# Low parts of the projections' weights: a subtraction on VectorE replaced by a negation on ScalarE and an accumulating transfer

## The chip, the cores and the metric

The kernel runs on one core of one Trainium2 chip. A core has a TensorE (PE, matrix products into PSUM banks), a VectorE (DVE), a ScalarE (ACT), a GpSimd (POOL) and a SyncE (SP), each with its own in-order instruction queue, and 16 DMA engines. The metric is the device time of one execution in microseconds, as the median of several runs.

## The reference

One layer of a hybrid block over 1024 tokens of width 1024. Two branches read the same RMS-normalised input; their gated sum is projected and added to the input, and a squared-ReLU MLP and a last RMSNorm follow.

```python
xn = rmsnorm(x, norm1_g[layer])
u = xn @ w_in[layer].astype(f32)
q_sb, k_sb, v_sb, f_raw, i_hg, q_hg, g_hg, gate_sb, gate_hg = jnp.split(u, list(c), axis=-1)
o_sb = stick_breaking_attention(split_heads(q_sb, SB_HEADS), ...)
...
o_hg = hgrn2_chunkwise(split_heads(jax.nn.silu(q_hg), HG_HEADS), ...)
...
merged = g_a * (o_sb @ w_o_sb[layer].astype(f32)) + g_b * (o_hg @ w_o_hg[layer].astype(f32))
h = x.astype(f32) + merged @ w_out[layer].astype(f32)
hn = rmsnorm(h, norm2_g[layer])
a = jnp.square(jax.nn.relu(hn @ w_ff1[layer].astype(f32)))
h = h + a @ w_ff2[layer].astype(f32)
```

Everything is float32, and the tolerance is that of float32.

## The kernel before

The large products are made in a rounded float32 format (`fp32r`). To keep the precision, each operand is split into a high part (the value rounded to that format) and a low part (the rest), and every product is made of three matmuls, high by high, high by low and low by high (`three`, line 466). The high part is a copy on ScalarE that rounds (`hi_copy`, line 133, recorded as L134). The low part is a subtraction on VectorE, raw minus high (`lo_sub`, line 136, recorded as L137). `hi_lo` (line 139) does both.

The weights of the projections come in units (class `Unit`, line 368). `Unit.load` (line 378) has SP load one or two raw tiles of 128x1024 float32 (512 KB) from HBM; `Unit.split` (line 390) makes a high and a low tile of each. The raw tiles lie in a pool with two buffers of the tag `raw`; high and low tiles of the narrow units have two buffers each (`whi`, `wlo`), those of the wide units (value, input and w_out projections) lie in the general slots. So a raw buffer can be loaded again only when the unit's split has read it, and a high or low buffer can be written again only when the matmuls of the unit two before have read it.

Jobs are queued in a `Stream` (line 413): the first job makes queries and keys of head 0 and the values of heads 0 to 3 (`first_job`, line 580); then come queries and keys of heads 1 to 7 (`wqk1` to `wqk7`, with `wv1` between), the recurrence's projections (`wf`, `wq`, `wi`, `wg` per head), 16 gate projections (`wg00` to `wg17`) with an output projection of the attention or the recurrence after every second one (`wo00` to `wo13`), and two jobs of w_out (`wout_job`, line 1035). When a job starts, `Stream.prefetch` (line 431) splits the next job's unit and loads the one after it. The tiles of a unit are named after it with h, l and r behind: `wo13h`, `wo13l`, `wo13r`.

The matmuls of the jobs fill the gaps of the main work on PE, whose order against the jobs is written out by hand: stick-breaking attention up to about 320 us (scores z, sigmoids `rm` and `bt`, a scan on VectorE at line 646, a product `bt`, transposes `pw`, their split into `wTh` and `wTl`, and the values `po`), then the levels and tails of the recurrence; from wg06 on the jobs run alone. In attention each head's queries are copied to the other half of the partitions by two DMAs issued from POOL (line 563, QH<-QH and QL<-QL). POOL also writes the small memsets at lines 631 and 676. A scheduler that knows the dependencies sets each engine's final order.

The tail of the kernel is the MLP, which makes its splits elsewhere and does not use `Unit`.

Of the kernel before, what the change touches and what calls it, by code (L numbers as in the profile page):

```python
# [14 lines left out]
ALU = mybir.AluOpType  # L15
# [24 lines left out]
def kernel(  # L40
# [19 lines left out]
    nc = tc.nc  # L60
# [14 lines left out]
    def slot(name, dt=F32):  # L75
        return spool.tile([P, 1024], dt, tag="s", name=name)
# [7 lines left out]
    def bank(name):  # L84
        return psum.tile([P, 512], F32, tag="p", name=name)
# [3 lines left out]
    class Lane:  # L89
        def __init__(self):  # L90
            self.ends = []
            self.last = None
            self.gates = ()
# [4 lines left out]
    def after(ins, earlier):  # L98
        if earlier is not None and earlier.ins is not ins.ins:
            tc.add_manual_dep(ins.ins, earlier.ins.name, NOSYNC, reason="issue order")  # L100
        return ins
# [26 lines left out]
    def load(dst, src):  # L128
        last_load[0] = after(nc.sync.dma_start(dst, src), last_load[0])
# [3 lines left out]
    def hi_copy(dst, src):  # L133
        after(nc.scalar.copy(dst, src), hold[0])  # L134

    def lo_sub(dst, src, hi):
        return nc.vector.tensor_tensor(out=dst, in0=src, in1=hi.bitcast(F32), op=ALU.subtract)  # L137

    def hi_lo(h, l, src):
        hi_copy(h, src)  # L140
        return lo_sub(l, src, h)
# [134 lines left out]
    class Quads:  # L276
# [42 lines left out]
        def split(self, i, kp, src, pr=0, n=4):  # L319
            if (i, kp) not in self.hl:  # L320
                self.hl[i, kp] = tuple(slot(f"sq{n_}{i}{kp}", F32R) for n_ in "hl")
            h, l = (self.part(t, pr, n) for t in self.hl[i, kp])
            self.last_lo = hi_lo(h, l, self.part(src, pr, n))
# [44 lines left out]
    class Unit:  # L368


        def __init__(self, name, pieces, wide=False):
            self.name = name
            self.pieces = pieces
            self.wide = wide
            self.raw = None
            self.hl = None

        def load(self):
            if self.raw is not None:
# [10 lines left out]
        def split(self):  # L390
            if self.hl is not None:
                return
            self.load()
            self.hl = []
            for i, r in enumerate(self.raw):
                if self.wide:
                    h = slot(f"{self.name}h{i}", F32R)
                    l = slot(f"{self.name}l{i}", F32R)
                else:
                    h = wpool.tile([P, 1024], F32R, tag="whi", name=f"{self.name}h{i}")  # L400
                    l = wpool.tile([P, 1024], F32R, tag="wlo", name=f"{self.name}l{i}")
                hi_lo(h, l, r)
                self.hl.append((h, l))

    def cols_unit(name, parts):

        dmas, c = [], 0
        for mat, c0, n in parts:
            dmas.append((c, n, mat[:, c0 : c0 + n].rearrange("(k p) c -> p k c", p=P)))
            c += n  # L410
        return Unit(name, [dmas])
# [54 lines left out]
    def three(ps, wh, wl, xh, xl, first, last, goes_on=False):  # L466
        matmul(ps, wh, xh, start=first, stop=False, skip_group_check=goes_on)
        matmul(ps, wh, xl, start=False, stop=False, skip_group_check=goes_on)
        matmul(ps, wl, xh, start=False, stop=last, skip_group_check=goes_on)

    def proj_half(ps, hl, mov, nk, half, wcol=lambda k: k * P):
        wh, wl = hl
        for kt in range(nk):
            c = wcol(kt)
            xh, xl = mov(kt, half)
            three(ps, wh[:, c : c + P], wl[:, c : c + P], xh, xl, kt == 0, kt == nk - 1)
            if kt % 2 == 1:
                yield
# [13 lines left out]
    def token_steps(name, unit, acts, tbs, epilogue):  # L492

        for tb in tbs:
            ps = bank(f"{name}_{tb}")[:, 0:256]
            for kt in range(KT):
                sh, sl = acts.stat(kt, tb)
                wh, wl = unit.hl[kt // 4]
                cs = slice((kt % 4) * 256, (kt % 4 + 1) * 256)
                three(ps, sh, sl, wh[:, cs], wl[:, cs], kt == 0, kt == KT - 1)  # L500
                if kt == 3:
                    yield
            epilogue(ps, tb)
            yield
# [31 lines left out]
    def v_epilogue(quad):  # L536


        def ep(ps, tb):
            if tb % 2 == 0:  # L540
                vt[quad, tb // 2] = slot(f"V{quad}_{tb // 2}", F32R)
            V = vt[quad, tb // 2].rearrange("p (t h s d) -> p t h s d", t=2, h=4, s=2)
            src = ps.rearrange("p (h d) -> p h d", h=4)
            hi_lo(V[:, tb % 2, :, 0, :], V[:, tb % 2, :, 1, :], src)

        return ep
# [20 lines left out]
    def v_unit(quad):  # L567
        return wide_unit(f"wv{quad}", W_IN, C_V + quad * 256)
# [7 lines left out]
    def qk_item(h):  # L576
        u = cols_unit(f"wqk{h}", [(W_IN, C_Q + h * DHS, DHS), (W_IN, C_K + h * DHS, DHS)])
        return f"pjqk{h}", u, qk_epilogue(h)

    def first_job():  # L580
        name, u_qk, ep = qk_item(0)
        u_v = v_unit(0)

        def body():
            v_ep = v_epilogue(0)
            for half in range(2):
                ps = bank(f"{name}_{half}")
                yield from proj_half(ps, u_qk.hl[0], xn.mov, KT, half)
                ep(ps, half)
                if half == 0:  # L590
                    u_v.split()
                    yield
                    st.prefetch()
                yield from token_steps("pjv0", u_v, xn, range(4 * half, 4 * half + 4), v_ep)

        return st.add([u_qk, u_v], body)

    j_qk = {0: first_job()}
    for h in range(1, NHS):
        j_qk[h] = proj_jobs([qk_item(h)], xn)  # L600
# [164 lines left out]
    for h in range(NHG):  # L765
        for key, c0, ep in (
# [6 lines left out]
            u = cols_unit(f"w{key}{h}", [(W_IN, c0 + h * P, P)])  # L773
# [229 lines left out]
    for which in range(2):  # L1003
        for cp in range(4):
            for cb in (2 * cp, 2 * cp + 1):
                c0 = (C_GA, C_GB)[which] + cb * P
                u = cols_unit(f"wg{which}{cb}", [(W_IN, c0, P)])
# [27 lines left out]
    def wout_job(n):  # L1035
        cs = slice(n * 512, (n + 1) * 512)
        units = [
            Unit(
                f"wout{n}{i}",
                [[(0, 512, W_OUT[i * 256 : (i + 1) * 256, cs].rearrange("(k p) c -> p k c", p=P))]],  # L1040
                wide=True,
            )
            for i in range(4)
        ]

        def body():
            for tb in range(NT):
                if n == 0:
                    hres.append(slot(f"h{tb}"))
                    load(hres[tb], X[tb * P : (tb + 1) * P, :])  # L1050
                    if tb in AHEAD_AT:
                        st.prefetch()
                ps = bank(f"pw{n}_{tb}")
                for kt in range(KT):
                    sh, sl = mgs.stat(kt, tb)
                    wh, wl = (w[:, kt % 2 * 512 : (kt % 2 + 1) * 512] for w in units[kt // 2].hl[0])
                    three(ps, sh, sl, wh, wl, kt == 0, kt == KT - 1)
                nc.vector.tensor_tensor(
                    out=hres[tb][:, cs], in0=hres[tb][:, cs], in1=ps, op=ALU.add
                )  # L1060
                yield

        return st.add(units, body)

    AHEAD_AT = (2, 4, 6)
    for n in range(2):
        j_wout = wout_job(n)
# [388 lines left out]
    for i, it in enumerate(items):  # L1456
# [8 lines left out]
        r = turn(*it)  # L1465
# [137 lines left out]
```

## Time and profile before

| | us |
|---|---|
| median of 3 runs | 1520.06 (1518.52 to 1520.98) |
| the profiled execution | 1516.4 |
| its span, first to last instruction | 1514.6 |
| PE busy / DVE busy / ACT busy / POOL busy | 1483.2 / 962.1 / 616.2 / 69.1 |

Stretches of the span, with the busy time of each engine in them:

```profile
110.00:140.00 30.00, 27.41 (x168) 23.84 (x167) 28.27 (x35) 22.15 (x48) 4.70 (x21) 1.00 0.42 95
244.00:264.00 20.00, 19.06 (x107) 16.28 (x107) 16.57 (x23) 12.95 (x28) 0.90 (x8) 1.00 0.27 80
632.00:785.00 153.00, 153.00 (x677) 126.69 (x676) 49.35 (x60) 39.08 (x51) 0.00 (x0) 1.00 0.17 52
```

The columns are the stretch, its length, then busy time and number of instructions of PE, PE's weight loads, DVE, ACT and POOL, the granted clock of PE, the share of the DMA engines that is busy, and GB/s. A matmul of 512 columns is recorded with 0.39 us but the next one starts 0.23 us after it: they overlap in the array, and a busy PE is one with no gap between such records. The engine that waits is named first in a list of waits, then what it waited for, the sum in us, how often, and the longest.

### The profile page before, as it was taken

How to read it: one execution, taken by the hardware profiler on the slowest of the kernel's cores; microseconds unless marked ns; L12 is line 12 of the kernel's file. 1: busy time of each engine (PE TensorE's matmuls, PEld its weight loads, DVE VectorE, ACT ScalarE, POOL GpSimd, SP SyncE). 2: the span in 40 equal slices, each digit the busy share in tenths (PEclk: the TensorE clock that was granted, in tenths of full speed). 3: DMA queues.
4: the chain of work that ended last, by engine and by line, in shares of the span. 5: the costliest groups of instructions: out<-in, count | busy, mean ns of one | idle time of the engine just before them, and what ended most of it. 6: DMA issues, size and time to landing. Idle time of an engine off the chain costs nothing.

```text
span 1514.6 us, 19739 instructions
## 1 busy us (share of the span) xinstructions
PE 1483.2 (98%) x7677; PEld 1258.7 (83%) x7677; DVE 962.1 (64%) x1379; ACT 616.2 (41%) x1091; POOL 69.1 (5%) x242
## 2 busy tenths in 40 slices
PE   7999999999999999999999999999999999999997
PEld 6888988988898888888888888888888878888886
DVE  5689798786535554232344479766666857757765
ACT  6566566541312211222232275444444434443433
POOL 2011010000000000000000000000000000000020
PEclk9999999999999999999999999999999999999999
DMA  7123012001101011111115232344444996654744
GB/s 202 29 56 77 8 53 67 15 15 43 57 1 42 29 38 33 42 56 42 56 56 195 111 107 96 127 153 152 153 153 153 341 374 250 222 202 172 260 141 170
DMA packets 125716, 172.21 MB, mean 114 GB/s; under 512 B 22924, under 2 KB 76216, under 8 KB 125624
## 3 DMA queue, kind: packets, MB, share of 16 engines
q1 hardware_dynamic: 124088, 166.77, 32.2%
q0 software_dynamic: 1536, 4.20, 1.2%
q8 instruction: 60, 0.98, 0.3%
q14 instruction: 32, 0.26, 0.0%
HBM read 129.00 MB, written 37.75 MB: 110 GB/s over the span
## 4 chain that ended last, share of the span: by engine, by line
PE 77%; DVE 5%; issue 5%; ACT 2%; DMA 2%; POOL 1%; SPq 0%; POOLq 0%; DVEq 0%; ACTq 0%
PE pm L121 15%; PE pjg L121 14%; PE pX L121 8%; PE py L121 6%; PE pY L121 5%; PE pW L121 5%; PE pw L121 4%; PE sl L121 3%; PE pjf L121 3%; PE pji L121 3%; PE pjq L121 2%; PE po L121 2%; PE pjv L121 1%; DVE rm L646 1%; PE z L121 1%
## 5 line engine op out<-in xcount | busy, mean ns | idle before, releaser
L134 ACT CAST whid<-w 128x1024 fp32r<-128x1024 f32 x31 | 32.7, 1055 | 166.7 <-PE pm L121 114.9
L646 DVE TENSOR_TENSOR_SCAN rm<-rm,bits 128x895 f32<-128x895 f32 (+5 forms) x64 | 86.1, 1349 | 18.8 <-ACT rm L627 17.1
L121 PE MATMUL pm<-whid,sl 128*128 128x512 f32 x248 | 96.6, 389 | 0.7 <-DVE sl L137 0.7
L121 PE MATMUL pm<-whid,sh 128*128 128x512 f32 x248 | 96.6, 390 | 0.6 <-ACT sh L134 0.6
L121 PE MATMUL pm<-wlod,sh 128*128 128x512 f32 x248 | 96.5, 389 | 0.0
L121 PE MATMUL pm<-th,sl 128*128 128x512 f32 x200 | 77.9, 390 | 0.4 <-DVE sl L137 0.4
L121 PE MATMUL pm<-tl,sh 128*128 128x512 f32 x200 | 77.8, 389 | 0.0
L121 PE MATMUL pm<-th,sh 128*128 128x512 f32 x200 | 77.8, 389 | 0.0
L137 DVE TENSOR_TENSOR sl<-sa,sh 128x1024 fp32r<-128x1024 f32 x56 | 68.3, 1220 | 2.0 <-ACT sh L134 2.0
L137 DVE TENSOR_TENSOR wlod<-w,whid 128x1024 fp32r<-128x1024 f32 x31 | 37.9, 1224 | 39.9 <-ACT whid L134 39.6
L134 ACT CAST wTh<-pw 128x128 fp32r<-128x128 f32 (+3 forms) x96 | 44.0, 484 | 45.9 <-PE pw L124 42.8
L134 ACT CAST sh<-sa 128x1024 fp32r<-128x1024 f32 x56 | 57.9, 1049 | 3.4 <-DMA sa<-ad 3.2
L121 PEld LDWEIGHTS pm<-whid,sl 128*128 128x128 f32 x248 | 46.5, 188 | 10.8 <-DVE sl L137 1.2
L121 PEld LDWEIGHTS pm<-whid,sh 128*128 128x128 f32 x248 | 46.6, 188 | 10.7 <-ACT sh L134 1.0
L137 DVE TENSOR_TENSOR wTl<-pw,wTh 128x512 fp32r<-128x512 f32 (+3 forms) x96 | 50.5, 547 | 7.6 <-ACT wTh L134 4.5
L121 PEld LDWEIGHTS pm<-wlod,sh 128*128 128x128 f32 x248 | 46.5, 188 | 9.6
L121 PEld LDWEIGHTS sl<-q,k 128*128 128x128 f32 (+1 forms) x448 | 50.2, 184 | 2.9 <-issue 1.1
L144 DVE TENSOR_TENSOR bt<-bt,rm 128x895 f32<-128x895 f32 (+5 forms) x64 | 48.2, 755 | 5.0 <-ACT bt L630 0.3
L121 PE MATMUL sl<-q,k 128*128 128x128 f32 (+1 forms) x448 | 51.3, 268 | 0.0
L964 ACT ACTIVATE g<-pjg,prm 128x512 f32<-128x512 f32 x32 | 21.9, 686 | 71.7 <-PE pjg L121 71.7
L121 PE MATMUL pX<-sqh,t1l 128*128 128x512 f32 x128 | 49.9, 390 | 0.5 <-DVE t1l L137 0.5
L627 ACT ACTIVATE rm<-z 128x511 f32<-128x511 f32 (+6 forms) x96 | 47.3, 500 | 7.6 <-DVE bt L144 4.5
(798 smaller groups left out, 4398.6 us busy)
## 6 DMA issues: line engine op xcount, KB each, us to landing
w<-in_w_ff_dram SPq DMA_DIRECT2D x72, 512.0 KB, 4.5
sa<-ad SPq DMA_DIRECT2D x56, 512.0 KB, 6.9
ad<-a SPq DMA_DIRECT2D x32, 256.0 KB, 3.8
ad<-s SPq DMA_DIRECT2D x16, 512.0 KB, 3.3
x<-in_x_dram SPq DMA_DIRECT2D x8, 512.0 KB, 4.5
h<-in_x_dram SPq DMA_DIRECT2D x8, 512.0 KB, 8.0
hd<-h SPq DMA_DIRECT2D x8, 512.0 KB, 2.7
ad<-p SPq DMA_DIRECT2D x16, 256.0 KB, 4.5
```

Of the source, the lines that this page charges most:

```text
L121: return pe(nc.tensor.matmul(*a, **k))
L134: after(nc.scalar.copy(dst, src), hold[0])
L137: return nc.vector.tensor_tensor(out=dst, in0=src, in1=hi.bitcast(F32), op=ALU.subtract)
L144: nc.vector.tensor_tensor(out=out, in0=a, in1=b, op=ALU.mult)
L627: nc.scalar.activation(rm[:, s0 + c0 - 1 : s0 + m - 1], z[:, c0:m], AF.Sigmoid, scale=-0.125)
L646: nc.vector.tensor_tensor_scan(out=rr, data0=rr, data1=bits[:, 1024 - nk : 1023][:, ::-1], initial=0.0, op0=ALU.mult, op1=ALU.max,)
L964: nc.scalar.activation(dst, ps, AF.Sigmoid, bias=b)
```

## The change

Where a unit is not marked urgent, its low part is no longer subtracted on VectorE. ScalarE writes the negated, rounded raw tile into the low tile (the target's format rounds it, so it is minus the high part), and POOL issues a DMA that adds the raw tile to what stands in the low tile: raw minus high. The high part is made as before. The units of the first job and of w_out are marked urgent and keep the subtraction.

```diff
         def __init__(self, name, pieces, wide=False):
...
             self.hl = None
+            self.urgent = False
...
-                hi_lo(h, l, r)
+                hi_copy(h, r)
+                if self.urgent:
+                    lo_sub(l, r, h)
+                else:
+                    nc.scalar.mul(l, r, -1.0)
+                    nc.gpsimd.dma_start(l, r, accum_op=ALU.add)
                 self.hl.append((h, l))
...
+        u_qk.urgent = u_v.urgent = True
         return st.add([u_qk, u_v], body)
...
+        for u in units:
+            u.urgent = True
         return st.add(units, body)
```

The transfer reads the raw tile, so the raw buffer is free for the next load when the transfer has landed, and the matmuls that read the low tile wait for the same landing.

## The prediction

> **What bounds the kernel now.** I read the page's busy shares and its chain first: TensorE (PE) is busy 98% of the span, and the chain that ended last is 77% PE. VectorE (DVE) at 64% and ScalarE (ACT) at 41% matter only where PE waits for them.
>
> ```profile
> span 1514.6 us, 19739 instructions
> PE 1483.2 (98%) x7677; PEld 1258.7 (83%) x7677; DVE 962.1 (64%) x1379; ACT 616.2 (41%) x1091; POOL 69.1 (5%) x242
> ```
>
> Next, PE's waits in the attention stretch (50 to 350 us); the same view for 600 to 800 us is empty. The chain of waits over the same stretch then says how those waits come about.
>
> ```profile
> PE po L121 <- DVE wTl L137: 3.6, 4, 1.4
> PE pw L124 <- DVE bt L144: 1.9, 2, 1.1
> PE pjv L121 <- DVE QL L137: 0.9, 1, 0.9
> PE pjv L121 <- DVE wTl L137: 0.3, 1, 0.3
> ```
> ```profile
> 126.79 1.12 DVE wqk5l L137
> ...
> 135.58 1.22 DVE wqk6l L137
> ...
> 251.22 1.23 DVE wi0l L137
> 252.47 3.61 DMA wg0r<-in_w_in_dram
> 256.10 1.06 ACT wg0h L134
> ```
>
> So all that PE loses to VectorE there is 6.7 us, and three low-part subtractions are links of the chain. At 252 us the chain also passes through a load that waits for a raw buffer: a subtraction ends at 252.4, only then is the buffer free, the load takes 3.61 us, and ScalarE, in order, stands at the copy behind it until 256.1.
>
> Last, how long before its first use a low part is ready. I asked for every unit's tiles; the tightest stretch is 632 to 785 us, one job of 48 matmuls after the other. Its last unit:
>
> ```profile
> L121 PEld LDWEIGHTS py<-ahgh,wo13l x16: 187/188/188, 784.5 to 794.7; 128*128 128x128 f32 x16
> ...
> L137 DVE TENSOR_TENSOR wo13l<-wo13r,wo13h x1: 1226/1226/1226, 774.5 to 774.5; 128x1024 fp32r<-128x1024 f32 x1
> ```
>
> The rounding copy wo13h starts at 773.4 (it waits for the buffer that PE reads until then); the low part is first needed at 784.5. That is 11.1 us, and the 15 units from wg06 to wo13 have 11.1 to 11.7; every other unit has 13 us or more.
>
> **The change, part by part.** The instruction order of the changed kernel shows 49 tiles moved (7 wqk, 2 wv1, 12 wf/wq/wg, 4 wi, 16 gate, 8 output); first job and w_out keep the subtraction. The order of the matmuls is the same but for a few places after 380 us.
>
> *Removed:* 49 subtractions of 128x1024 on VectorE, 1.22 us each (row L137 wo13l): 60 us. *Added:* 49 negations on ScalarE; the nearest row is the 128x1024 ACTIVATE of line 224, 1.06 us: 52 us. *Added on POOL:* 49 DMA issues; the issue of QH<-QH takes 0.52 us: 25 us at least on a queue busy 69 us. *Added to the DMA engines:* 49 times 512 KB, read twice over (raw piece and target). After 350 us PE waits for neither engine, so none of these sums counts by itself; what counts is the delay until the low part lands.
>
> *Landing time X, from POOL's issue.* The trace has no accumulating transfer. Its rows for landing:
>
> ```profile
> QH<-QH POOLq DMA_DIRECT2D x16, 128.0 KB, 2.3
> ...
> hb<-hd SPq DMA_DIRECT2D x8, 512.0 KB, 9.7
> ```
> ```profile
> wo10r<-in_w_o_hg_dram SPq DMA_DIRECT2D x1, 512.0 KB, 3.4
> ```
>
> From 2.3 us for 128 KB and 3.4 for 512 KB, 384 KB cost 1.1 us, so 512 KB are 1.5 us on a fixed 1.9. Lower bound 3.4 (as if a plain copy), upper bound 9.7 (the slowest 512 KB row, in a full queue). I take the payload twice, since target and raw piece are both read: 1.9 + 2 x 1.5 = 4.9 us; the queue is nearly empty here, so it is nearer to the 3.4 row than to 9.7. The Trainium skill, page "Collectives: The Full Stack", section "Why 7× under link rate", states that an adding transfer runs at half a copy's rate because it has two source reads; by that rule X is the same 4.9, and without it, at a copy's rate, 3.4. No row here shows which.
>
> *The tight stretch.* On ScalarE the order becomes rounding copy (1.05), mostly the sigmoid of the job just ended (L964, 0.69), negation (1.06): 2.8 us. Plus 0.3 from ScalarE's end to POOL's issue (as between QH's copy and its issue at 46.16). Of 11.1 us, 8.0 are left for X. With 4.9 the low part is 3.1 us early: cost 0. The cover is exactly this 8.0: beyond it every job waits. There are two low-part buffers, so a delay e stretches two job periods at once and costs e/2 per job, 15 times.
>
> *115 to 138 us.* VectorE has no idle time from 110.8 to 138.4; four moved subtractions (two wv1l, wqk5l, wqk6l: 4.8 us) lie in it, and PE's waits there are 1.4 (po on wTl), 0.3 and 0.9 (pjv): 2.6. ScalarE is busy 22.15 of the 30 us from 110 to 140 and gets 4.2. I take 2.0 of the 2.6 back: -2.0 (bounds -2.6 and +2).
>
> *248 to 266 us.* The raw buffer of wi0's first half is now freed by the transfer. Negation from 251.35 (behind bt's evacuation) to 252.4, issue at 252.7, landing at 257.6, load 3.6: the copy wg0h starts at 261.2 in place of 256.1. In the new order it stands six instructions later, ahead of wTh (0.6) and the bt pair (1.1), which end at 263.9; VectorE's product of 1.2 us ends at 265.1, and PE's transposes of it began at 264.27: +0.8. The instructions that now run before the copy free wTl, for which PE waited 0.9 us at 260.7: -0.9. Together -0.1; with X at 8.0 it is +3.0, with 3.4 -0.9.
>
> *POOL's queue.* The transfers of wqk2l and later ones now stand ahead of the QL<-QL copies. For head 0 QL is issued at 47.64; behind the transfer (issued at 47.2) it lands by about 52.8, and z first needs it at 55.1: 0, but +2.4 if X is 9.7. The one-column memsets queued behind it are used microseconds later: 0. SP's loads wait for raw buffers 3 to 6 us longer; outside 252 us each has a job of slack.
>
> **Sum.** -2.0 - 0.1 = -2.1 us. The profiled execution took 1516.4 us (span 1514.6 and 1.8 around it), so it would be 1514.3; the median shown is 1520.06, 3.7 above the profiled one, and the same difference gives **1518.0**. The forecast's own range, from the bounds of its terms, is 1514 to 1523. A difference under 0.2% (3.0 us) can hardly be told from none here.
>
> **Rivals.**
> 1. *The transfers land too late* (the other side). Place: the 15 jobs from 632 us. It decides from X = 8.0. At 9.7: (9.7 - 8.0)/2 x 15 = 12.8, at 252 us 4.8 more, head 0's QL 2.4: 1518.0 + 20.0 = 1538. At 12 us it would be 30 us for the jobs alone. For: no accumulating transfer was ever seen here, the software queue shares its engines with SP's loads, and single QH landings reach 6.2 us. Against: the stretch moves only 52 GB/s.
> 2. *ScalarE takes VectorE's place in attention.* In the new order, ten of the 17 negations before 345 us stand directly ahead of a wTh copy, on which wTl and po hang. All ten exposed: 10 x 1.06 = 10.6 us; about six of them, and nothing recovered: 1526. For: VectorE waited 17.1 us for ACT's rm, 4.5 for its wTh. Against: ScalarE idles 42.8 us before wTh copies, waiting for PE, so most negations fall into idle time.
> 3. *It is hidden anyway.* VectorE's gain is eaten by the next wait in line (wTl after wTh), and the 252 us place breaks even: 1520, no change.
>
> **Chances.** Forecast 0.46 (0.20 of it more than 3 us faster, 0.24 within, 0.02 slower); rival 1 0.24 and rival 2 0.18, both slower; rival 3 0.12, no change. So faster 0.20, same 0.36, slower 0.44. The time is that of the likeliest case. The range 1514 to 1536 leaves out some 4% below (all of attention's waits gone) and 13% above (X of 10 us and more).
>
> **What would show it.** X right: the tiles' landing rows at about 5 us, and still no PE wait between 632 and 785 us. Wrong: PE waiting there on a DMA into a gate or output unit's low part, about once per job. The 115 to 138 us step: PE's waits on wTl and QL gone or replaced by waits behind ACT. The 252 us step: the copy wg0h starting near 261 us, and a PE wait of a microsecond near 265. VectorE's busy time falls by 60 us and ScalarE's rises by 52, or the costs per instruction were wrong. What would make the forecast wrong as a whole is X above 8 us.

## The result and the profile after

The changed kernel takes 1523.73 us (median of 7 runs, 1522.31 to 1528.53) against 1520.06 for the kernel before (7 runs, 1517.38 to 1521.22). The ratio is 1.0032 with a 95% interval of 1.0018 to 1.0046: slower by 3.7 us in the medians and 4.9 by the ratio, where 2.1 us less were forecast. The profiled execution took 1523.47 us, close to its median, so its trace can be read for the loss. The one of before (1516.4) lies 3.7 us under its median, and part of the 7.0 us between the two spans is that luck.

The page of the changed kernel, its first lines and the queue of GpSimd's transfers (packets, MB, share of 16 engines):

```profile
span 1521.6 us, 19842 instructions
PE 1484.9 (98%) x7677; PEld 1259.7 (83%) x7677; DVE 906.3 (60%) x1330; ACT 660.9 (43%) x1140; POOL 112.1 (7%) x291
...
q0 software_dynamic: 8592, 29.89, 10.2%
```

VectorE lost 55.8 us of work, ScalarE gained 44.7 and GpSimd 43.0; PE is as busy as before. So nothing became a bound by its sum. The list of PE's waits from 50 to 350 us (sum, times, longest):

```profile
PE pw L124 <- DVE bt L144: 5.0, 3, 3.1
PE pjv L121 <- DVE wTl L137: 1.9, 1, 1.9
PE po L121 <- DVE wTl L137: 1.3, 2, 1.1
```

The waits for low parts fell from 4.8 us (3.6, 0.9, 0.3) to 3.2, but a third wait for the product bt, of 3.1 us, has come in, where PE did not wait before. The list for 600 to 800 us is empty, as before. The chain of waits in the changed kernel, where that wait arises:

```profile
256.37 1.09 ACT rm L635 x2
257.46 0.04 ACT wTh L134
257.50 5.05 DMA wg0r<-in_w_in_dram
...
262.57 0.03 ACT wg0h L134
262.60 0.93 issue
263.52 0.58 ACT wTh L134
264.10 0.99 ACT bt L638 x2
...
265.12 1.24 DVE bt L144
266.36 0.04 issue
266.40 1.97 PE pw L124 x8
268.37 1.46 PE po L121 x8
```

The load of wg0r starts at 257.50, when the first transfer of wi0 has landed (issued at 252.88). ScalarE has nothing to do that it may do: the next instruction of its queue is the copy of wg0r, and wTh and the bt pair of the attention stand behind it. Its own list of waits says the same, and names a second, smaller place of the kind at wqk5:

```profile
ACT wg0h L134 <- DMA wg0r<-in_w_in_dram: 4.6, 1, 4.6
ACT wqk5h L134 <- DMA wqk5r<-in_w_in_dram: 2.9, 1, 2.9
```

What the wait leaves behind shows in two stretches of 3 us (busy PE, its weight loads, DVE, ACT, POOL, then PE's granted clock):

```profile
264.00:267.00 3.00, 0.60 (x3) 0.60 (x4) 2.54 (x4) 2.95 (x7) 0.00 (x0) 0.83 0.04 10
267.00:270.00 3.00, 3.00 (x18) 3.00 (x17) 2.43 (x2) 2.15 (x6) 1.28 (x5) 0.60 0.45 87
```

Clocks of 0.83 and 0.60, where the kernel before has 1.00. From the start of the first transpose behind the wait (266.40 us, before 264.11) to that of the first score behind it PE takes 3.26 us, before 1.82: the wait of 3.1 us costs 1.4 us more after it has ended.

Second, the end of the kernel. The instructions of the program's last line, first of the kernel before and then of the changed one (shortest, median and longest in ns; first and last start):

```profile
L1598 POOLq DRAIN  x3: 102/188/3296, 1508.9 to 1514.2; - x3
L1598 SPq DRAIN  x3: 7/7/7, 1513.3 to 1513.6; - x3
```
```profile
L1608 POOLq DRAIN  x3: 40/158/7297, 1513.1 to 1521.3; - x3
L1608 SPq DRAIN  x3: 7/7/7, 1517.5 to 1521.0; - x3
```

GpSimd's drain begins at 1508.9 and takes 3.3 us before: it ends at 1512.2, while SP still waits for the last output until 1513.3. In the changed kernel it takes 7.3 us, ends at 1520.4, and every other engine has been done since 1517.6. From the last matmul to the end of the span it is 12.0 us, before 9.2: another 2.8 us.

Where the time went, as the start of the same matmul in several kernels minus that in before (each from its own span's start; the runs are described below, "repair 1" is f1, "both" g1, "three" g2, "control" g3):

| | before, us | changed | repair 1 | both | three | control |
|---|---|---|---|---|---|---|
| first product of wqk0 | 17.6 | +0.6 | +0.3 | 0.0 | +2.2 | +2.3 |
| first of wqk4 | 112.5 | +0.6 | +0.3 | 0.0 | +2.2 | +2.3 |
| first of wqk5 | 170.6 | -0.1 | -0.8 | -1.0 | -0.4 | +1.2 |
| first of wq0 | 248.6 | -0.1 | -0.8 | -1.0 | -0.3 | +1.2 |
| first of wi0 | 268.4 | +3.8 | -1.7 | -1.9 | -1.3 | +0.3 |
| last of wo13 | 794.9 | +3.3 | -2.2 | -2.4 | -1.7 | +0.3 |
| first th by sl of the MLP | 1204.3 | +3.3 | -2.2 | -2.4 | -1.8 | +0.4 |
| last matmul | 1505.4 | +4.2 | -2.1 | -0.6 | -1.4 | +1.5 |
| from there to the end | 9.2 | 12.0 | 12.0 | 8.7 | 8.8 | 9.2 |

The first row and the step from 1204 to 1505 us differ between runs of the same code there (0.0 to 2.3 us, and 0.1 to 5.3 us over all runs), so a single profile says nothing by them. The second goes with the clock: e2, f3, f4, f5 and g1 have 3.4 to 6.8 us at half clock near 1225 us and lose 1.8 to 5.3 us from 1204 to 1505 us, the runs without such a stretch 0.1 to 1.5. Between them the changed kernel loses 2.7 us: it gains 0.7 at 112 to 171 us, loses 3.8 at 249 to 268, and gains 0.5 later. With the 2.8 of the end that is 5.5 us, inside the interval of the ratio.

### The profile page after: what moved, and what is told of

The parts are those of the page before. It is cut to its first block, busy times and chain, and to the rows that moved or that the text cites. A ratio compares the mean times of both kernels' runs of the same rounds, so it can differ in the third digit from the quotient of the medians.

```text
span 1521.6 us, 19842 instructions
## 1 busy us (share of the span) xinstructions
PE 1484.9 (98%) x7677; PEld 1259.7 (83%) x7677; DVE 906.3 (60%) x1330; ACT 660.9 (43%) x1140; POOL 112.1 (7%) x291
## 4 chain that ended last, share of the span: by engine, by line
PE 86%; issue 5%; DVE 4%; ACT 2%; DMA 2%; POOL 1%; POOLq 0%; SPq 0%; DVEq 0%; ACTq 0%
PE pm L121 16%; PE pjg L121 14%; PE pX L121 8%; PE py L121 6%; PE pY L121 6%; PE pW L121 5%; PE pw L121 4%; PE pjqk L121 4%; PE sl L121 3%; PE pjv L121 3%; PE pjf L121 3%; PE pji L121 3%; PE pjq L121 3%; PE po L121 2%; PE pw L124 2%
## 5 line engine op out<-in xcount | busy, mean ns | idle before, releaser
L144 DVE TENSOR_TENSOR g<-py,g 128x512 f32<-128x512 f32 x16 | 11.0, 688 | 74.5 <-PE py L121 74.5
L121 PE MATMUL pX<-sql,t1h 128*128 128x512 f32 x128 | 50.0, 391 | 0.3 <-DVE sql L137 0.3
```

The costliest lines, as they stand in the source:

```text
L121: return pe(nc.tensor.matmul(*a, **k))
L144: nc.vector.tensor_tensor(out=out, in0=a, in1=b, op=ALU.mult)
```

## The experiments

Two theories. H: the raw buffer of a wide unit is held until its transfer lands, the next load comes late, and ScalarE, in order, stands at the copy behind it. D: GpSimd's last drain grows with the transfers that it issued. Rivals: A, the additional work of ScalarE; T, the traffic and landing of the transfers; L, the tight jobs from 632 us. Ratios are to the kernel before on the same chip, with 95% intervals.

**h0, the changed kernel again.**

> The changed kernel again, on the chip of these runs, as their yardstick: 0.3% over before; a wait pw <- bt of 3 us near 264 us with the clock at half behind it, and a last drain of 7.3 us on GpSimd, as in its first profile. If either of the two were chance in that one profile, it would be missing here.

Measured: 1523.72 us, ratio 1.0026 (1.0015 to 1.0037); the wait is 3.1 us, the clock dips behind it, the drain takes 7.3 us. Neither was chance.

**e1, wi0 subtracts again.**

```diff
-                if self.urgent:
+                if self.urgent or self.name == "wi0":
```

> The changed kernel, but wi0 alone (2 of the 49 tiles) keeps VectorE's subtraction, so its raw buffers come free early again. Theory H (the raw buffer of wi0 is held until the transfer lands, the load of wg0r comes 5 us late, ScalarE stands in order at the copy wg0h, PE waits 3.1 us and then runs 3.4 us at half clock): wg0h starts near 256 to 257 us, PE's wait pw <- bt of 3.1 us near 264 us is gone, the clock is 1.00 in 250 to 300 us, and the time falls by 3.5 to 5 us against the changed kernel, to 1518.5 to 1520.5, equal to before or up to 1.5 us faster. Rival A (ScalarE's additional 45 us of negations cost by themselves, spread over the attention) and rival T (the 49 transfers and their landing cost by themselves): 47 of 49 tiles are unchanged, so the time stays within 1 us of 1523.7.

Measured: 1523.07 us, 1.0030 (1.0018 to 1.0042). A miss for the number of theory H, though its signs came: wg0h starts at 257.1 us, the 3.1 us wait and the dip are gone, and from the first row of the table above to the MLP the run loses 0.2 us and not 2.7. The time hardly fell. This run led to the drain: its end takes 11.9 us, 47 of 49 transfers being still there. The remaining 1.5 us or so are within the interval.

**e2, wi0 alone is changed.**

```diff
-                if self.urgent:
+                if self.urgent or self.name != "wi0":
```

> The other half of the pair: only wi0 (2 tiles) uses negation and transfer, the other 47 tiles keep the subtraction. Theory H: nearly the whole loss is there with 2 tiles, PE waits 3 us near 264 us with a lower clock after it, the time is 1523 to 1525 (before plus 3 to 5). Rivals A and T: 2/49 of the loss, 0.2 us, so 1520 (before, within 0.5).

Measured: 1524.54 us, 1.0034 (1.0023 to 1.0046). Two of the 49 tiles are enough for the loss near 264 us, so rivals A and T do not explain it. The wait is 3.5 us, the clock 0.50 for 6.8 us behind it, and 249 to 268 us lose 5.4 us, more than the 3.8 of the changed kernel. The end takes 8.7 us: 34 transfers of GpSimd, a drain of 3.5. So this loss has no part of the drain's, and that the two ratios are alike is chance.

**e3, the negations alone.**

```diff
                     nc.scalar.mul(l, r, -1.0)
-                    nc.gpsimd.dma_start(l, r, accum_op=ALU.add)
+                    lo_sub(l, r, h)
```

> All 49 negations stay on ScalarE, but the low part is then overwritten by VectorE's subtraction as in the kernel before; no transfer is issued. ScalarE has its 45 us more, VectorE none less, POOL and the DMA engines nothing more. The raw buffer is held by about 1 to 2 us longer than before (a negation) instead of about 6. Rival A: the loss of 3.7 us or more is there (1523.5 to 1526), with VectorE's subtraction also waiting for the negation. Theory H: within 2 us of before, 1519 to 1522, and no PE wait over 1.5 us near 264 us; the copy wg0h starts at 257 to 258.

Measured: 1517.34 us, 0.9989 (0.9981 to 0.9998). ScalarE's 49 negations cost nothing, with VectorE's subtractions behind them: rival A is out. The kernel even gains 1.2 us at 112 to 171 us, without any relief of VectorE; the order of the instructions there changed, but that this is the reason is not shown.

**e4, another buffer for wg0's raw tile.**

```diff
-                r = wpool.tile([P, 1024], F32, tag="raw", name=f"{self.name}r{i}")
+                if self.name == "wg0":
+                    r = slot(f"{self.name}r{i}")
+                else:
+                    r = wpool.tile([P, 1024], F32, tag="raw", name=f"{self.name}r{i}")
```

> The changed kernel, all 49 transfers kept, but the raw tile of wg0 lies in a general slot and not in the two raw buffers, so its load need not wait for wi0's transfer. Theory H: the load of wg0r starts before 252 us, ScalarE does not stand at the copy wg0h (its idle of 4.6 us there is gone), the PE wait of 3.1 us near 264 us and the half clock are gone: 1518 to 1520. If a slot comes free only late the wait moves to the slot, and the time stays. Rivals A and T: all negations and transfers are still there, 1523 to 1525.

Measured: 1524.64 us, 1.0038 (1.0025 to 1.0050). Inconclusive: the load is issued at 250.3 us and ScalarE's idle time at the copy is gone, as H says, but the scheduler, which plans with the early load, put the copy and the negation of wg0 ahead of a wTh and of the rm sigmoids, and the product bt starts only at 266.2. The wait was 2.8 us, with the same dip. It suggests that the place in ScalarE's queue is what counts, which f1 tests by itself.

**f1, the order alone.** The copy and the negation of wg0 are put behind the last bt sigmoid issued before them:

```diff
-                hi_copy(h, r)
+                keep, hold[0] = hold[0], lastbt[0] if self.name == "wg0" else hold[0]
+                hi_copy(h, r)
+                hold[0] = keep
...
-                    nc.scalar.mul(l, r, -1.0)
+                    after(nc.scalar.mul(l, r, -1.0), lastbt[0] if self.name == "wg0" else None)
```

> The changed kernel with all 49 transfers; only the two ScalarE instructions that read wg0's raw tile (rounding copy wg0h and negation wg0l) are ordered behind the last bt sigmoid issued before them in the program, which puts them some 25 places later in ScalarE's queue. The raw buffer of wi0 is held as long, and the load of wg0r comes as late, as in the changed kernel; only nothing of the attention stands behind it. Theory H (in-order ScalarE standing at the copy is what costs): its idle of 4.6 us at wg0h is gone, the wait pw <- bt of 3.1 us near 264 us falls to 1 us or less, the clock stays 1.00 from 250 to 300 us; 4 us less than the changed kernel, so 1519 to 1520.5. Rival A (the negations on ScalarE) or rival T (traffic of the transfers slows the attention): nothing changes there, 1523 to 1524.5. Either way the end of the kernel keeps the long GpSimd drain of theory D (7.3 us).

Measured: 1520.62 us, 1.0003 (0.9994 to 1.0012). PE's waits of this run from 50 to 350 us, and its stretch behind 264 us:

```profile
PE pw L124 <- DVE bt L144: 1.9, 2, 1.1
PE pjv L121 <- DVE wTl L137: 1.8, 1, 1.8
PE po L121 <- DVE wTl L137: 1.3, 2, 1.1
```
```profile
264.00:267.00 3.00, 3.00 (x20) 2.61 (x19) 2.81 (x4) 2.79 (x8) 0.01 (x1) 1.00 0.01 3
```

The copy runs at 276.3 us, 28 us before its use; the transfers, the held buffer and the negations are all as they were. The wait and the dip are gone, and with them 3.1 us by the medians and 4.4 by the ratios. With its control f2 (below) that shows theory H.

**f3, a drain in the middle.**

```diff
-                    nc.gpsimd.dma_start(l, r, accum_op=ALU.add)
+                    d = nc.gpsimd.dma_start(l, r, accum_op=ALU.add)
+                    if self.name == "wo13":
+                        after(nc.gpsimd.drain(), d)
```

> The changed kernel with one more instruction: a drain on GpSimd directly behind the last of the 49 transfers (near 780 us), where GpSimd has nothing else to do. Theory D (the drain of GpSimd at the end takes 3.3 us with 32 issued transfers, 7.3 us with 81, and its last 2.9 us come after every other engine is done): if a drain pays for the transfers issued up to it, the last one falls to 3.3 us or less and the time by 2.5 to 2.9 us against the changed kernel, to 1520.8 to 1521.3; if the last drain pays again for all transfers of the kernel, the time stays at 1523.7 and the drain at 7.3 us. Theory H alone: 1523.7, and the stretch from the last matmul to the end has no part in the loss.

Measured: 1521.18 us, 1.0012 (1.0003 to 1.0021). The drain put in, and the drains at the end:

```profile
L411 POOLq DRAIN  x1: 7926/7926/7926, 780.5 to 780.5; - x1
...
L1610 POOLq DRAIN  x3: 34/102/656, 1515.8 to 1520.7; - x3
```

The 7.9 us are paid at 780 us, where GpSimd has nothing to do, and the last long drain shrinks to 0.66 us; from the last matmul to the end it is 8.7 us in place of 12.0. Theory D holds, as a loss of its own.

**f4, transfers in the late units alone** (16 gate and 8 output units; the attention's units subtract).

```diff
-                if self.urgent:
+                if self.urgent or not (self.name[:3] in ("wg0", "wg1") and len(self.name) == 4 or self.name[:2] == "wo"):
```

> Negation and transfer only for the 24 gate and output units (after 350 us), the 25 tiles of the attention stretch keep VectorE's subtraction. Theory H: no transfer is in the attention stretch, so the waits of PE up to 350 us are those of before (6.7 us in all, clock 1.00). Theory D: 56 transfers of GpSimd in all, so its last drain takes 3.3 + 24 x 0.082 = 5.3 us, of which about 0.8 to 1 lies behind the other engines: 1 us slower than before, 1519.5 to 1520.5. Rival L (the tight stretch from 632 us costs after all): PE waits there, and the time is 1523 or more.

Measured: 1518.93 us, 0.9999 (0.9990 to 1.0007). Rival L is out: 24 transfers in the jobs from 350 us on, the tight ones among them, cost nothing. The drain takes 5.25 us as expected, from 1515.1 to 1520.3 us, and SP is done at 1519.4: the drain ends last, by 0.9 us. The end still takes 9.1 us, as before, because SP was done 0.4 us sooner after the last matmul than in the other profiles (7.5 for 7.9 us) and what follows the last engine took 0.8 us for 1.3. So some of the drain may be exposed here, 0.4 to 0.9 us; the time does not show it.

**f5, 49 small transfers in the kernel before.**

```diff
+                if self.name[:2] in ("wg", "wo") and len(self.name) == 4:
+                    for j in range(3 if self.name == "wo13" else 2):
+                        c = 2 * nt[0]
+                        nc.gpsimd.dma_start(tiny[:, c : c + 2], l[0:1, c : c + 2].bitcast(F32))
+                        nt[0] += 1
```

> The kernel before, all subtractions on VectorE, no negations; added are 49 copies of 8 bytes each issued by GpSimd in the stretch after 350 us, from low tiles that are already written; the order of all other engines is that of before. It measures theory D by itself. If the last drain counts transfers, it takes 7.2 us as with 81, and the time is that of before plus 2.5 to 2.9 us, 1521.5. If it counts bytes or packets (the 49 tile transfers brought 7056 packets), the drain stays at 3.3 to 3.6 us and the time is that of before.

Measured: 1521.30 us, 1.0015 (1.0006 to 1.0024). With 81 transfers in all, 49 of them of 8 bytes, the last drain is as long as with the tiles, and from the last matmul to the end it is 11.6 us:

```profile
L1605 POOLq DRAIN  x3: 40/98/7298, 1515.0 to 1522.8; - x3
```

It counts transfers, not bytes: 3.30 us with 32, 3.45 with 34, 5.25 with 56, 7.13 with 79, 7.30 with 81, so 4.0 / 49 = 0.082 us for each, and 0.66 are left with none (f3).

**f2, the order alone in the kernel before** (the same edit around its `hi_lo`).

> The kernel before with wg0's rounding copy ordered behind the last bt sigmoid issued before it (its subtraction follows the copy). Control for the run that did the same to the changed kernel. ScalarE's 3.3 us at the copy behind the load of wg0r, and PE's wait of 0.9 us for wTl at 260.7 us behind it, go: 0.9 us less than before (1519). If the gain of that run came from the order alone and had nothing to do with the held raw buffer, this one would be about 4 us faster than before (1516).

Measured: 1517.25 us, 0.9989 (0.9981 to 0.9998); by its trace 249 to 268 us gain 0.9 us, as expected. In the changed kernel the same edit gains 4.7 us there (a loss of 3.8 becomes a gain of 0.9), so 3.8 of it undo what the transfer does.

**g1, both repairs; g2, and wqk5's copy and negation behind a bt sigmoid too.**

```diff
-                keep, hold[0] = hold[0], lastbt[0] if self.name == "wg0" else hold[0]
+                keep, hold[0] = hold[0], lastbt[0] if self.name in ('wqk5', 'wg0') else hold[0]
...
-                    after(nc.scalar.mul(l, r, -1.0), lastbt[0] if self.name == "wg0" else None)
+                    after(nc.scalar.mul(l, r, -1.0), lastbt[0] if self.name in ('wqk5', 'wg0') else None)
```

> Both repairs together in the changed kernel: wg0's copy and negation behind the bt sigmoid, and a drain of GpSimd behind the last transfer. Theories H and D as two separate losses: 4.4 us (half of it and more the wait, the rest the clock after it) and 2.9 us, so 7.3 less than the changed kernel, 1516.5 to 1517.5, 0.15 to 0.25% under before; the last drain under 1 us, no clock dip at 266 us. If they were one loss seen twice: 1519.5 to 1520.5, as with the first repair alone.

> As the run with both repairs, and the copy and the negation of wqk5 (ScalarE stands 2.9 us at that copy near 126 us behind the raw buffer that wv1's transfer holds) are ordered behind a bt sigmoid too. Theory H at this second place: PE's wait pjv <- wTl of 1.9 us at 132.6 us goes, 0.5 to 1.5 us less than the run with both repairs, 1515.5 to 1516.5. If the scheduler's other order there brings a wait of its own, no gain or a loss of up to 2 us.

Measured: g1 1515.64 us, 0.9983 (0.9973 to 0.9993); g2 1515.43 us, 0.9971 (0.9961 to 0.9981). The two losses add up, and g2 is the best version of the study: 0.3% under the kernel before and 0.55 to 0.6% under the changed one. PE's waits of g2 from 50 to 350 us, 3.5 us in place of 6.7 before:

```profile
PE pw L124 <- DVE bt L144: 1.9, 2, 1.1
PE po L121 <- DVE wTl L137: 1.3, 2, 1.1
PE pjv L121 <- DVE wTl L137: 0.3, 1, 0.3
```

**g3, g2's order without any transfer** (the kernel before, wqk5 and wg0 behind a bt sigmoid).

> The kernel before, all subtractions on VectorE, no transfer, with the rounding copies of wqk5 and wg0 ordered behind a bt sigmoid as in the run with three repairs. If the order alone makes that run's gain: 1515.5 as well, within 1 us of it. If relieving VectorE is worth the 2 us of the forecast by itself: only the gain of the control (1517 to 1518), since ScalarE did not wait at wqk5h in the kernel before, so 1.5 to 2.5 us slower than the run with three repairs, and PE's waits po <- wTl of 1.4 us and pjv <- QL of 0.9 us between 115 and 138 us are still there.

Measured: 1517.40 us, 0.9986 (0.9977 to 0.9995). From the first product to the MLP it gains 1.9 us and g2 3.9, so relieving VectorE is worth 2 us by the trace and 0.15% by the times, though the intervals of the two overlap a little (up to 0.9981, from 0.9977). At 112 to 171 us it is 1.1 of order against 2.6 with the relief. The order gains there although ScalarE did not wait at wqk5h before, which was not expected: PE's wait po <- wTl of 1.4 us is still there, but pjv <- QL of 0.9 us is gone.

**e6, the same transfers as plain copies.** The low parts hold the raw weights here; the subtraction is left out.

```diff
-                    nc.gpsimd.dma_start(l, r, accum_op=ALU.add)
+                    nc.gpsimd.dma_start(l, r.bitcast(F32R))
```

> The changed kernel with the same 49 transfers as plain copies instead of additions; the low parts then hold the raw weights instead of raw minus high, so the output is not the reference's. By the rule of two source reads a plain copy lands sooner than the 4.6 us of the adding transfer: 1.9 + 1.5 = 3.4 us. If the adding costs nothing and the 4.6 us are those of any 512 KB transfer between tiles from this queue, the landing stays at 4.5 to 4.6 us and PE's wait of 3.1 us near 264 us too.

Measured: 1517.05 us, one run. Landing rows and the queue from 600 to 800 us, first of the changed kernel, then of this one:

```profile
q0 software_dynamic: 2433, 8.85, 23.2%
...
wo13l<-wo13r POOLq DMA_DIRECT2D x1, 512.0 KB, 4.5
```
```profile
q0 software_dynamic: 2304, 8.39, 11.4%
...
wo13l<-wo13r POOLq DMA_DIRECT2D x1, 512.0 KB, 2.9
```

The adding transfer lands 1.6 us later, and a megabyte takes 2.6% of the engines' time in these 200 us against 1.4%: twice as much. The rule of the Trainium skill, page "Collectives: The Full Stack", section "Why 7× under link rate", that a transfer which adds runs at half a copy's rate because it reads two sources (the page says it of a collective's ReduceScatter), agrees with this. The 1.6 us decide: at 2.9 us the copy wg0h starts at 257.4 us and the 3.1 us wait does not arise. From the first product to the MLP this run is 4.1 us shorter than the kernel before, with neither copy moved, so both places, wqk5 and wg0, hang on how long the transfer holds the raw buffer.

## Why the prediction was wrong

**Bounds, landing time, tight stretch: right.** X was forecast at 4.9 us, and 512 KB land in 4.5 to 4.6 us in most places (6.2 for the second transfer of wi0, beside the first). The second payload was put at 1.5 us and costs 1.6 (e6); a plain copy between tiles lands in 2.9 us, not in the 3.4 of the lower bound. No job from 632 us waited, so rival 1 did not come, and f4 shows it alone. The sums of work were right within 20% for VectorE (55.8 for 60 us) and ScalarE (44.7 for 52). Rival 2 named the engine on which it went wrong, but not the cause: ScalarE's work costs nothing (e3), its standing still does. Rival 3 was not the case either.

**115 to 138 us, forecast -2.0: right in kind, swallowed in part.** The changed kernel gains 0.7 us there. PE's waits fell from 2.6 to 1.9 and not to 0.6: ScalarE stood 2.9 us at wqk5h behind the buffer that wv1's transfer holds. The prediction saw that the loads wait 3 to 6 us longer, but gave each of them, outside 252 us, a job of slack; here there was none. With that place mended (g2) the stretch gains 2.6, of which 1.1 come from the order alone (g3).

**248 to 266 us, forecast -0.1: the step that failed, by 3.9 us.** Its mechanism is what the trace shows; its terms were mis-sized. The first landing came as forecast (257.6; the load was issued at 257.50), by two small errors that nearly cancel: the issue came 0.2 us later and the landing took 0.3 us less. The load took 5.05 us and not 3.6: the second transfer of wi0, issued at 254.5, was under way beside it. The runs bear this out: the same load takes 4.9 to 5.1 us beside such a transfer (e2, f3 and the changed kernel) and 3.6 to 3.9 without one (before, e1, f4) or beside a plain copy (e6). So the copy came at 262.57 for 261.2, and bt ended at 266.36 for 265.1: 1.3 us. Then the 0.9 us gained at 260.7 was booked as if it reached the end. It did not: PE came earlier by what had been gained before, and met a wait whose end ScalarE sets, and a gain ahead of such a wait only makes it longer, so the sum's own +0.8 should have stood without the -0.9. Last, the step had no term for the clock after the wait, 1.4 us. These three are 3.6 of the 3.9 us.

**POOL's queue, forecast 0: the term that was missing.** The step looked at who waits behind the transfers in the middle of the kernel, and not at what GpSimd owes at its end. The added issues were counted (25 us at least, 43 measured) and the drain, 3.3 us with 32 transfers in the trace of before, was not carried to 81: +2.8 us.

The three steps were off by 1.3, 3.9 and 2.8 us; less the 0.5 us gained after 268 us, this is the way from the -2.1 forecast to the +5.5 of the trace, within 0.1.

That g1 ends near the forecast time does not bear the forecast out: it has two edits that the forecast did not have, and 0.9 us of its gain come from an order that the kernel before can have as well (f2). What the runs do support is the worth of relieving VectorE, forecast at 2.0 us: the traces of g2 and g3 differ by 2 us.

## What to carry to other kernels

When a subtraction in an engine becomes a transfer, the source buffer is held until it lands: look for the load that waits for this buffer, then for the in-order engine that stands at that load's first reader, and move this reader back in the queue, or let the buffer go sooner. Count a gain only up to the next wait whose end something else sets. Transfers issued by GpSimd leave a bill at the end of the program, which a drain in an idle stretch pays.

## What the runs showed of the hardware

- GpSimd's last drain takes 0.66 us, and 0.082 us more for each transfer that it issued since the drain before, whatever their size. With 32 transfers (3.3 us) it ended 1.1 us before SP was done, with 56 (5.25 us, f4) 0.9 us behind it, with 81 (7.3 us) 2.9 us behind it.
- After PE waits of 2.8 to 3.5 us near 264 us the granted clock was 0.5 for 3.4 us (6.8 after the longest), and the waits of 1.4 us and less in the kernel before left it at 1.00. Shorter waits do not always leave it there: two in a row near 1225 us, of 0.9 to 1.2 us (2.4 in f5) and 0.7 us, were followed by half clock in e2, f3, f4, f5 and g1, and two of 1.3 and 0.7 us in the changed kernel were not. The Trainium skill, page "TensorE: Matmul & The Clock Gate", section "HAM oscillation — how this bites in real kernels", names gaps over about 3.4 us as the ones to avoid; here 2.8 us (e4) and 3.1 us were enough.
- An adding transfer of 512 KB between tiles lands in 4.5 us, a plain one in 2.9. GpSimd's issue of the adding one takes 0.85 to 0.97 us, that of the plain one mostly 0.53 to 0.62 (e6) and that of 8 bytes 0.50 to 0.62 (f5), so it is the adding and not the size that makes it longer.
- The load of wg0r, 512 KB from HBM, took 4.9 to 5.1 us beside an adding transfer and 3.6 to 3.9 without one.
